# The last two steps of a triangular inverse: two chunks at a time, and six chunks at a time in one tile

## The chip, the cores and the metric

One core of a Trainium2 chip runs the whole program in one launch. The metric is the device time of an execution in microseconds (us). Before the change it is 3433.0 us, the median of three runs (3425.45, 3433.0 and 3433.71).

## The reference, cut to what matters

The reference is one layer of a hybrid encoder: RMSNorm, one wide projection `p = h @ w_in`, two recurrent mixers that share its columns, an output projection, a convolutional gated feed-forward part, a last RMSNorm. It runs over 2048 frames behind 16 meta tokens (one stream with zero state), and over 8 short streams of 16 frames with given states.

The change lies in the first mixer, RWKV-7 with 8 heads of 64. Per head and frame:

```python
def step(S, inp):
    r_t, k_t, v_t, w_t, kk_t, a_t = inp
    sa = jnp.einsum('bhvk,bhk->bhv', S, -kk_t)
    S = (S * w_t[:, :, None, :] + sa[..., None] * (kk_t * a_t)[:, :, None, :]
         + v_t[..., None] * k_t[:, :, None, :])
    return S, jnp.einsum('bhvk,bhk->bhv', S, r_t)
```

Taken 64 frames at a time (a chunk), the frames of a chunk depend on each other through a 64x64 triangular matrix L of products between keys, and the chunk needs the inverse of (1 + L). The reference never forms it; the kernel does.

## The kernel before, in words

**Layout.** The 2192 frames are split into segments: segment 0 has 272 (the eight short streams, the meta tokens and 128 frames), segments 1 to 5 have 384 each. A segment passes through the mixers in four units; a unit is one pair of RWKV heads (and beside it one head of the second mixer, mLSTM). A pair of heads fills the 128 partitions, 64 for each. So there are 24 units in all. A unit of segments 1 to 5 has six chunks, in three groups `cgroups` of two; a unit of segment 0 has five, of which the first group, the short streams, needs no last steps of the inverse.

**One unit.** `rwkv` makes the projections (`proj`, whose matmuls are line 322: 128x128 weights against 384 columns in float32r, three products for each of eight slices), the scores (tiles `scs`, line 710 to 733), and then the inverse. Its diagonal blocks of 16x16 are inverted on GpSimd (POOL, lines 751 to 760), go to memory and come back as the tile `ct`; lines 766 to 773 spread them into `TA`, six writes on POOL. `TA[:, 0]` holds the inverse so far and `TA[:, 1]` its transpose. Then `levels` (line 786) doubles the block size twice, 16 to 32 and 32 to 64, with the off-diagonal part of L masked into `cL`:

* `pi` = cL x TA0 (`mmd`: line 307, two matmuls of 64x64x64, one for each half of the partitions, each recorded as two instructions since they are float32),
* `wv` = a copy of `pi` out of PSUM, on VectorE (DVE),
* `pj` = TA1 x wv and, for the first doubling, also its transpose wv x TA1,
* TA = TA - pj, on DVE (line 804).

At its end line 808 applies the finished inverse to the chunk's keys and values (`pp`), and ScalarE (ACT) puts the result into `scs` (line 810). Then the chunks run one after another through the state `Z[u]` (lines 815 to 853, matmuls of lines 824, 837 and 843; the new state is line 841). In the code `levels` of a group stands ahead of that group's chunks and behind those of the group before.

**What sets the order.** A planner places the instructions of all engines by a priority that follows the order in the code, shifted by the offsets that `ranked`/`rank` add (`lev` adds 30, and -800 in segment 0), and by its own simulation of when each is ready. Each engine then runs its list in order. The chain of a unit (levels, chunks) is written out at the start of the next unit, ahead of that unit's front (`pend`, `at("chain")`), so the planner lays it between the next unit's projections.

**What is shared.** PSUM has eight banks; the tag `iv` has two. `pi`, `pj` and `pp` take them in turn, and so do the transposes of mLSTM (`m_T`, line 943) and those of the RWKV output (line 868). `TA` has three buffers of two chunks, `cL` and `wv` two each. POOL also issues the loads of the cached weights (line 372).

Of the kernel before, what the change touches and what calls it, by code (L numbers as in the profile page):

```python
# [211 lines left out]
def trunk_kernel(ctx: ExitStack, tc: tile.TileContext, A):  # L212
# [29 lines left out]
    def move(name, out, src, scale=None, eng="S"):  # L242
        e = knob(name, eng)
        turn[name] = turn.get(name, 0) + 1
        e = e[turn[name] % len(e)]
        if e == "S":
            if scale is None:
                S.copy(out, src)
            else:
                S.activation(out, src, AF.Copy, scale=scale)  # L250
        elif scale is None:
            (V if e == "V" else G).tensor_copy(out, src)
        else:
            (V if e == "V" else G).tensor_scalar(out, src, scale, None, op0=ALU.mult)

    def tt(name, out, a, b, op, eng="G"):
        e = knob(name, eng)
        turn[name] = turn.get(name, 0) + 1
        (V if e[turn[name] % len(e)] == "V" else G).tensor_tensor(out, a, b, op=op)  # L259
# [12 lines left out]
    def C(n, rows=128):  # L272
        o, w = COFF[n]
        return cst[:rows, o:o + w]
# [30 lines left out]
    def mmd(out, lhsT, rhs, start=True, stop=True):  # L305
        for h in (0, 64):
            T.matmul(out[h:h + 64], lhsT[h:h + 64], rhs[h:h + 64], start=start, stop=stop)  # L307
# [81 lines left out]
    def pt(tag, shape=(128, 512)):  # L389

        tag = knob("t_" + tag, tag.split("_")[0])
        t = psp.tile([128, 512], F32, name="ps_" + tag, tag=tag, bufs=banks[tag])[:, :math.prod(shape[1:])]
        if len(shape) == 2:
            return t
        return t.rearrange("p (a b) -> p a b", b=shape[2]) if len(shape) == 3 else t.rearrange("p (a b c) -> p a b c", b=shape[2], c=shape[3])

    with p1:
# [220 lines left out]
        def rwkv(u, s, ws, h, lo1, lo2):  # L618
# [127 lines left out]
            with rank("inv"):  # L746
                bt = sp.tile([48, 16, 16], F32, name="bt", tag="bt", bufs=1)
                nc.sync.dma_start(ad[:nch].rearrange("c p j -> p c j"), cm[:, :nch])
                nc.sync.dma_start(bt[:nb].rearrange("q i j -> q (i j)"), ad[:nch].rearrange("c (g i) j -> (c g) (i j)", i=16))
                tb = sp.tile([48, 2, 16, 16], F32, name="tb", tag="tb", bufs=1)  # L750
                tmp = sp.tile([48, 64], F32, name="ttmp", tag="ttmp", bufs=1)
                G.memset(tb[:nb, 0], 0.0)
                G.memset(tb[:nb, 0].rearrange("p i j -> p (i j)")[:, 0:256:17], 1.0)
                for j in range(15):
                    x, y = 15 - j, j + 1
                    tv = tmp[:nb, :x * y].rearrange("p (x y) -> p x y", y=y)
                    G.tensor_tensor(tv, bt[:nb, j, j + 1:].unsqueeze(2).to_broadcast([nb, x, y]),
                                    tb[:nb, 0, j, :y].unsqueeze(1).to_broadcast([nb, x, y]), op=ALU.mult)
                    G.tensor_tensor(tb[:nb, 0, j + 1:, :y], tb[:nb, 0, j + 1:, :y], tv, op=ALU.subtract)
                move("e_tb", tb[:nb, 1], tb[:nb, 0].rearrange("p i j -> p j i"), eng="G")  # L760
                td = dr.tile([2, nb, 256], F32, name=f"td{u}_{s}")
                nc.sync.dma_start(td[:].rearrange("a q e -> q a e"), tb[:nb].rearrange("p a i j -> p a (i j)"))
                ct = sp.tile([128, 2 * nch, 16], F32, name="ct", tag="ct", bufs=1)
                nc.sync.dma_start(ct, td[:].rearrange("a (c g) (i j) -> (g i) (a c) j", g=8, j=16))
                TAg = []
                for cg in cgroups:
                    TA = sp.tile([128, 2, 2, 64], F32, name="TA", tag="TA", bufs=KN.get("b_TA", 4))
                    TAg.append(TA)
                    k, c0 = len(cg), cg[0]
                    for a in range(2):  # L770
                        tt("e_TA", TA[:, a, :k].rearrange("p c (b j) -> p c b j", j=16),
                                        ct[:, a * nch + c0:a * nch + c0 + k].unsqueeze(2).to_broadcast([128, k, 4, 16]),
                                        C("seq4").unsqueeze(1).unsqueeze(3).to_broadcast([128, k, 4, 16]), ALU.mult)

            @ranked("chain")
            def chain():
# [4 lines left out]
                def sb(t, h):  # L781

                    return t[:, :, 64:320 if h else 192].rearrange("p c (j e) -> p c j e", j=2)[:, :, :, 0:64]

                @ranked("lev")
                def levels(cg, TA):
                    k, c0 = len(cg), cg[0]
                    if s > 0 or c0 > 0:
                        cL = sp.tile([128, 2, 2, 64], F32, name="cL", tag="cL", bufs=KN.get("b_cL", 2))
                        lev = C("lev").rearrange("p (l t) -> p l t", t=64)  # L790
                        for i, c in enumerate(cg):
                            tt("e_cL", cL[:, :, i], SC[c][:, 0:64].unsqueeze(1).to_broadcast([128, 2, 64]), lev, ALU.mult, eng="V")
                        for l in range(2):
                            pi = pt("iv", (128, 2, 2, 64))
                            for i, c in enumerate(cg):
                                mmd(pi[:, 0, i], cL[:, l, i], TA[:, 0, i])
                            wv = sp.tile([128, 2, 64], F32, name="wv", tag="wv")
                            move("e_wv", wv[:, :k], pi[:, 0, :k])
                            pj = pt("iv", (128, 2, 2, 64))
                            for i, c in enumerate(cg):  # L800
                                mmd(pj[:, 0, i], TA[:, 1, i], wv[:, i])
                                if l == 0:
                                    mmd(pj[:, 1, i], wv[:, i], TA[:, 1, i])
                            V.tensor_tensor(TA[:, :2 - l, :k], TA[:, :2 - l, :k], pj[:, :2 - l, :k], op=ALU.subtract)
                    pp = pt("iv", (128, 2, 128))
                    for i, c in enumerate(cg):
                        for h, hs in enumerate(HALF):
                            T.matmul(pp[hs, i], TA[hs, 0, i], sb(SC[c][hs].unsqueeze(1), h)[:, 0], start=True, stop=True)  # L808
                    for h, hs in enumerate(HALF):
                        move("e_pp", sb(SG[c0][hs, :k], h), pp[hs, :k].rearrange("p c (j d) -> p c j d", d=64), -1.0)  # L810

                for gi, cg in enumerate(cgroups):
                    levels(cg, TAg[gi])
                    smp = s == 0 and cg[0] == 0
                    for i, c in enumerate(cg):
                        sc = SC[c]
# [784 lines left out]
```

## Time and profile before

| | |
|---|---|
| median of three runs | 3433.0 us |
| the profiled execution's own time | 3429.68 us |
| its span in the trace | 3427.9 us |
| mean granted TensorE clock | 0.975 of full speed |
| busy share of the span | PE 97%, weight loads 89%, DVE 63%, ACT 35%, POOL 31% |

Times in the trace count from the start of the span. PE is TensorE's matmuls and PEld its weight loads. A matmul that follows another starts before that one has ended, so "busy" is not "at its peak": what a matmul costs is the step from its start to the start of the next. L307 is line 307 of the kernel. The mixers fill the span up to about 1900 us, the feed-forward part the rest.

### The profile page before, as it was taken

How to read it: one execution, taken by the hardware profiler on the slowest of the kernel's cores; microseconds unless marked ns; L12 is line 12 of the kernel's file. 1: busy time of each engine (PE TensorE's matmuls, PEld its weight loads, DVE VectorE, ACT ScalarE, POOL GpSimd, SP SyncE). 2: the span in 40 equal slices, each digit the busy share in tenths (PEclk: the TensorE clock that was granted, in tenths of full speed). 3: DMA queues.
4: the chain of work that ended last, by engine and by line, in shares of the span. 5: the costliest groups of instructions: out<-in, count | busy, mean ns of one | idle time of the engine just before them, and what ended most of it. 6: DMA issues, size and time to landing. Idle time of an engine off the chain costs nothing.

```text
span 3427.9 us, 62699 instructions
## 1 busy us (share of the span) xinstructions
PE 3330.3 (97%) x23700; PEld 3040.1 (89%) x23700; DVE 2151.2 (63%) x5475; ACT 1199.6 (35%) x2940; POOL 1059.2 (31%) x2408
## 2 busy tenths in 40 slices
PE   7999999999999999999999999999999999999998
PEld 6776887888888888888877999999999999999998
DVE  7777767666676676676665466657544557545454
ACT  5443435433343343334334333334222223222222
POOL 2432435434444434344341333333111113100002
PEclk9888999999999999999998999999999999999999
DMA  8753666455445545544643877775644445644445
GB/s 311 254 167 105 207 209 211 166 172 175 149 144 188 176 145 183 186 154 148 197 133 129 329 274 268 284 254 201 223 157 161 162 160 168 231 154 160 161 165 181
DMA packets 257150, 651.36 MB, mean 190 GB/s; under 512 B 73472, under 2 KB 139424, under 8 KB 217808
## 3 DMA queue, kind: packets, MB, share of 16 engines
q1 hardware_dynamic: 177768, 300.58, 27.4%
q0 software_dynamic: 35376, 225.64, 19.4%
q10 hardware_dynamic: 43704, 121.13, 9.1%
q8 instruction: 188, 3.08, 0.4%
q14 instruction: 114, 0.93, 0.1%
HBM read 491.33 MB, written 155.95 MB: 189 GB/s over the span
## 4 chain that ended last, share of the span: by engine, by line
PE 82%; DVE 8%; DMA 4%; ACT 2%; issue 2%; POOL 1%; SPq 0%; POOLq 0%; ACTq 0%; DVEq 0%
PE ps_gm L322 23%; PE ps_iv L1191 16%; PE ps_gm L1191 11%; PE ps_a L1191 8%; PE ps_m L1191 7%; PE ps_iv L307 2%; PE ps_a L710 2%; PE ps_ch L824 1%; PE ps_ch L843 1%; PE ps_ch L837 1%; PE ps_iv L808 1%; PE ps_m L953 1%; DMA xt<-in_x_dram 1%; PE ps_a L307 1%; PE ps_a L728 1%
## 5 line engine op out<-in xcount | busy, mean ns | idle before, releaser
L322 PE MATMUL ps_gm<-hhi,w 128*128 128x384 f32 (+1 forms) x2976 | 815.8, 346 | 7.2 <-DVE w L259 2.4
L322 PEld LDWEIGHTS ps_gm<-hhi,w 128*128 128x128 f32 x2976 | 543.0, 194 | 29.9 <-issue 5.5
L322 PE MATMUL ps_gm<-hlo,w 128*128 128x384 f32 (+1 forms) x1488 | 504.1, 339 | 3.0 <-DVE hlo L362 3.0
L1176 ACT CAST w<-wr 128x1024 fp32r<-128x1024 f32 (+3 forms) x180 | 166.6, 926 | 613.7 <-PE ps_iv L1191 533.1
L1191 PE MATMUL ps_iv<-gh,w 128*128 128x384 f32 (+1 forms) x1170 | 308.9, 329 | 3.9 <-ACT gh L1176 2.1
L1191 PE MATMUL ps_iv<-hs,w 128*128 128x384 f32 x1584 | 298.0, 336 | 2.6 <-DVE uu L1339 1.7
L322 PEld LDWEIGHTS ps_gm<-hlo,w 128*128 128x128 f32 x1488 | 288.8, 194 | 9.3 <-DVE hlo L362 3.4
L1191 PEld LDWEIGHTS ps_iv<-hs,w 128*128 128x128 f32 x1584 | 277.9, 188 | 4.2 <-DVE uu L1339 2.7
L1177 DVE TENSOR_TENSOR w<-wr,w 128x1024 fp32r<-128x1024 f32 (+3 forms) x180 | 199.3, 1107 | 110.4 <-ACT w L1176 107.2
L1191 PEld LDWEIGHTS ps_iv<-gh,w 128*128 128x128 f32 x1170 | 209.9, 188 | 5.1 <-ACT gh L1176 2.8
L1191 PE MATMUL ps_gm<-h,w 128*128 128x384 f32 x1056 | 202.7, 342 | 1.7 <-ACT p L1337 1.7
L1191 PE MATMUL ps_gm<-h2hi,w 128*128 128x384 f32 (+1 forms) x880 | 203.4, 315 | 0.1
L1277 DVE SCALAR_TENSOR_TENSOR ac<-ub,par,ac 128x384 f32<-128x384 f32 (+2 forms) x308 | 175.1, 601 | 31.5 <-ACT ac L1275 22.6
L1191 PE MATMUL ps_iv<-gw,w 128*128 128x384 f32 (+1 forms) x585 | 192.7, 329 | 1.9 <-POOL gw L1177 1.9
L1191 PEld LDWEIGHTS ps_gm<-h,w 128*128 128x128 f32 x1056 | 188.1, 189 | 2.1 <-ACT p L1337 2.0
L322 PE MATMUL ps_gm<-yhi,w 128*128 128x384 f32 (+1 forms) x640 | 168.5, 336 | 0.9 <-ACT yhi L361 0.7
L1425 DVE TENSOR_TENSOR x<-x,ps_iv 128x384 f32<-128x384 f32 (+1 forms) x160 | 84.4, 528 | 122.2 <-PE ps_iv L1191 121.2
L372 POOL DMA_DIRECT2D w<-wc x155 | 92.4, 596 | 222.2 <-PE ps_gm L322 176.4
L1191 PE MATMUL ps_m<-gh,w 128*128 128x384 f32 (+1 forms) x590 | 157.3, 329 | 0.0
L1191 PEld LDWEIGHTS ps_gm<-h2hi,w 128*128 128x128 f32 x880 | 150.9, 189 | 0.8 <-DVE w L1177 0.3
L1272 POOL COPY h_f<-ub 128x2 f32<-128x2 f32 x88 | 35.8, 406 | 366.1 <-DVE ub L1346 342.5
L1177 POOL TENSOR_TENSOR gw<-ac,gh 128x384 fp32r<-128x384 f32 x66 | 73.1, 1108 | 243.6 <-ACT gh L1176 243.6
(462 smaller groups left out, 7504.3 us busy)
## 6 DMA issues: line engine op xcount, KB each, us to landing
w<-wc POOLq DMA_DIRECT2D x155, 1024.0 KB, 5.3
wr<-ws SPq DMA_DIRECT2D x88, 512.0 KB, 4.2
w<-wg SPq DMA_DIRECT2D x44, 1024.0 KB, 6.7
wc<-w ACTq DMA_DIRECT2D x31, 1024.0 KB, 7.5
wr<-in_w_up_dram SPq DMA_DIRECT2D x52, 512.0 KB, 11.3
wg<-w ACTq DMA_DIRECT2D x22, 1024.0 KB, 6.9
ws<-ws POOLq DMA_DIRECT2D x44, 512.0 KB, 7.4
w<-wa SPq DMA_DIRECT2D x44, 512.0 KB
```

The lines of the kernel that those rows point to most:

```text
L307: T.matmul(out[h:h + 64], lhsT[h:h + 64], rhs[h:h + 64], start=start, stop=stop)
L322: T.matmul(ps, w, x, start=i == 0, stop=i == len(seq) - 1)
L372: nc.gpsimd.dma_start(w, WC[cache][:])
L710: T.matmul(psS[hs, i, X], kb[hs, X, cl(c)], ar[hs, h, :, cl(c)], start=True, stop=True)
L728: T.transpose(psT[:, j], src, ident)
L808: T.matmul(pp[hs, i], TA[hs, 0, i], sb(SC[c][hs].unsqueeze(1), h)[:, 0], start=True, stop=True)
L1176: S.copy(hi, src)
L1177: eng.tensor_tensor(lo, src, f32(hi), op=ALU.subtract)
L1191: ins = T.matmul(ps, l, r, start=start and i + j == 0, stop=stop and i == len(x) - 1 and j == 2, skip_group_check=not start)
L1272: G.tensor_copy(so_ffn[:, f, 8] if s == len(SEGS) - 1 else h_f[:, f], ub[:, n:n + 2])
L1277: V.scalar_tensor_tensor(av, view(i), PR("fw", i * 22 + f), av, op0=ALU.mult, op1=ALU.add)
L1425: V.tensor_tensor(X[s][:, d, :n], X[s][:, d, :n], p, op=ALU.add)
```

## The change

`TA` becomes one tile for all six chunks, with one buffer instead of three. `levels` is called once for a unit (in segment 0 once for its groups 1 and 2) and takes the two doublings for all chunks together: for each doubling `cL` is made by one instruction for each group, `pi` is one PSUM tile of up to six chunks, `wv` one copy of up to 384 columns. For the first doubling the two products go to two PSUM tiles, `first_` and `pj`, and two subtractions bring them into `TA`; the second has one. `cL` and `wv` have one buffer each. The application to keys and values is a function of its own, `apply`, called three times behind the doublings and, as the call stands inside `levels`, ahead of the first chunk; its instructions are the ones of before. The short streams' group calls `apply` alone.

```diff
--- before.py
+++ after.py
@@ -762,13 +762,11 @@
                 nc.sync.dma_start(td[:].rearrange("a q e -> q a e"), tb[:nb].rearrange("p a i j -> p a (i j)"))
                 ct = sp.tile([128, 2 * nch, 16], F32, name="ct", tag="ct", bufs=1)
                 nc.sync.dma_start(ct, td[:].rearrange("a (c g) (i j) -> (g i) (a c) j", g=8, j=16))
-                TAg = []
+                TA = sp.tile([128, 2, 6, 64], F32, name="TA", tag="TA", bufs=1)
                 for cg in cgroups:
-                    TA = sp.tile([128, 2, 2, 64], F32, name="TA", tag="TA", bufs=KN.get("b_TA", 4))
-                    TAg.append(TA)
                     k, c0 = len(cg), cg[0]
                     for a in range(2):
-                        tt("e_TA", TA[:, a, :k].rearrange("p c (b j) -> p c b j", j=16),
+                        tt("e_TA", TA[:, a, c0:c0 + k].rearrange("p c (b j) -> p c b j", j=16),
                                         ct[:, a * nch + c0:a * nch + c0 + k].unsqueeze(2).to_broadcast([128, k, 4, 16]),
                                         C("seq4").unsqueeze(1).unsqueeze(3).to_broadcast([128, k, 4, 16]), ALU.mult)
 
@@ -783,34 +781,52 @@
                     return t[:, :, 64:320 if h else 192].rearrange("p c (j e) -> p c j e", j=2)[:, :, :, 0:64]
 
                 @ranked("lev")
-                def levels(cg, TA):
-                    k, c0 = len(cg), cg[0]
-                    if s > 0 or c0 > 0:
-                        cL = sp.tile([128, 2, 2, 64], F32, name="cL", tag="cL", bufs=KN.get("b_cL", 2))
-                        lev = C("lev").rearrange("p (l t) -> p l t", t=64)
+                def levels():
+
+                    a = 2 if s == 0 else 0
+                    cs = slice(a, nch)
+                    lev = C("lev").rearrange("p (l t) -> p l t", t=64)
+                    for l in range(2):
+                        cL = sp.tile([128, 6, 64], F32, name="cL", tag="cL", bufs=1)
+                        for cg in cgroups:
+                            if cg[0] >= a:
+                                k = len(cg)
+                                tt("e_cL", cL[:, cg[0]:cg[0] + k], SG[cg[0]][:, :k, 0:64], lev[:, l:l + 1].to_broadcast([128, k, 64]), ALU.mult, eng="V")
+                        pi = pt("iv", (128, 6, 64))
+                        for c in range(a, nch):
+                            mmd(pi[:, c], cL[:, c], TA[:, 0, c])
+                        wv = sp.tile([128, 6, 64], F32, name="wv", tag="wv", bufs=1)
+                        move("e_wv", wv[:, cs], pi[:, cs])
+                        for x in range(2 - l):
+                            pj = pt("iv", (128, 6, 64))
+                            for c in range(a, nch):
+                                mmd(pj[:, c], *((wv[:, c], TA[:, 1, c]) if x else (TA[:, 1, c], wv[:, c])))
+                            if l == 0 and x == 0:
+                                first_ = pj
+                            elif l == 0:
+                                V.tensor_tensor(TA[:, 0, cs], TA[:, 0, cs], first_[:, cs], op=ALU.subtract)
+                                V.tensor_tensor(TA[:, 1, cs], TA[:, 1, cs], pj[:, cs], op=ALU.subtract)
+                            else:
+                                V.tensor_tensor(TA[:, 0, cs], TA[:, 0, cs], pj[:, cs], op=ALU.subtract)
+                    for cg in cgroups:
+                        if cg[0] >= a:
+                            apply(cg)
+
+                @ranked("lev")
+                def apply(cg):
+                        k, c0 = len(cg), cg[0]
+                        pp = pt("iv", (128, 2, 128))
                         for i, c in enumerate(cg):
-                            tt("e_cL", cL[:, :, i], SC[c][:, 0:64].unsqueeze(1).to_broadcast([128, 2, 64]), lev, ALU.mult, eng="V")
-                        for l in range(2):
-                            pi = pt("iv", (128, 2, 2, 64))
-                            for i, c in enumerate(cg):
-                                mmd(pi[:, 0, i], cL[:, l, i], TA[:, 0, i])
-                            wv = sp.tile([128, 2, 64], F32, name="wv", tag="wv")
-                            move("e_wv", wv[:, :k], pi[:, 0, :k])
-                            pj = pt("iv", (128, 2, 2, 64))
-                            for i, c in enumerate(cg):
-                                mmd(pj[:, 0, i], TA[:, 1, i], wv[:, i])
-                                if l == 0:
-                                    mmd(pj[:, 1, i], wv[:, i], TA[:, 1, i])
-                            V.tensor_tensor(TA[:, :2 - l, :k], TA[:, :2 - l, :k], pj[:, :2 - l, :k], op=ALU.subtract)
-                    pp = pt("iv", (128, 2, 128))
-                    for i, c in enumerate(cg):
+                            for h, hs in enumerate(HALF):
+                                T.matmul(pp[hs, i], TA[hs, 0, c], sb(SC[c][hs].unsqueeze(1), h)[:, 0], start=True, stop=True)
                         for h, hs in enumerate(HALF):
-                            T.matmul(pp[hs, i], TA[hs, 0, i], sb(SC[c][hs].unsqueeze(1), h)[:, 0], start=True, stop=True)
-                    for h, hs in enumerate(HALF):
-                        move("e_pp", sb(SG[c0][hs, :k], h), pp[hs, :k].rearrange("p c (j d) -> p c j d", d=64), -1.0)
-
-                for gi, cg in enumerate(cgroups):
-                    levels(cg, TAg[gi])
+                            move("e_pp", sb(SG[c0][hs, :k], h), pp[hs, :k].rearrange("p c (j d) -> p c j d", d=64), -1.0)
+
+                for cg in cgroups:
+                    if s == 0 and cg[0] == 0:
+                        apply(cg)
+                    elif cg[0] == (2 if s == 0 else 0):
+                        levels()
                     smp = s == 0 and cg[0] == 0
                     for i, c in enumerate(cg):
                         sc = SC[c]
```

## Rows read from the trace of the kernel before

**Rows 1.** The page, busy time of each engine, its share of the span and instructions.

```profile
PE 3330.3 (97%) x23700; PEld 3040.1 (89%) x23700; DVE 2151.2 (63%) x5475; ACT 1199.6 (35%) x2940; POOL 1059.2 (31%) x2408
```

**Rows 2.** Busy time by stretch: stretch, its length, engines, granted clock, DMA share, GB/s.

```profile
0.00:600.00 600.00, 557.17 (x4271) 456.93 (x4272) 438.01 (x1396) 261.63 (x737) 224.45 (x606) 0.91 0.61 209
600.00:1700.00 1100.00, 1084.20 (x8931) 925.11 (x8931) 734.55 (x2288) 410.64 (x1225) 455.55 (x1136) 0.99 0.52 167
1700.00:1900.00 200.00, 185.62 (x1538) 160.04 (x1537) 127.42 (x385) 81.11 (x214) 67.45 (x155) 0.93 0.45 145
1900.00:3428.00 1528.00, 1503.36 (x8967) 1498.00 (x8965) 851.25 (x1407) 446.19 (x764) 311.77 (x512) 0.99 0.59 205
```

**Rows 3.** Timeline of PE: start, length, engine, line, operation, tiles, count.

```profile
1343.60 0.68 PE L322 MATMUL ps_gm<-yhi,w 128*128 128x384 f32 x3
1344.22 0.45 PE L307 MATMUL ps_iv<-TA,cL 64*64 64x64 f32 x8
1344.60 0.45 PE L322 MATMUL ps_gm<-ylo,w 128*128 128x384 f32 x1
1344.88 0.34 PE L322 MATMUL ps_gm<-yhi,w 128*128 128x384 f32 x1
```

**Rows 4.** Timeline of PE, a batch behind other 64x64 work.

```profile
1354.96 0.60 PE L808 MATMUL ps_iv<-scs,TA 64*64 64x128 f32 x7
1355.29 0.50 PE L307 MATMUL ps_iv<-TA,cL 64*64 64x64 f32 x8
1355.72 0.55 PE L1016 MATMUL ps_m<-cst,nd 128*128 128x128 f32 x3
```

**Rows 5.** Timeline of PE, a batch of sixteen.

```profile
1329.30 0.33 PE L307 MATMUL ps_iv<-wv,TA 64*64 64x64 f32 x4
...
1329.69 0.28 PE L307 MATMUL ps_iv<-TA,wv 64*64 64x64 f32 x4
1329.91 0.33 PE L728 MATMUL ps_a<-cst,vm 128*128 128x128 f32 x1
```

**Rows 6.** Line 307 on PE, 1320 to 1372 us: count, shortest/median/longest ns, first, last.

```profile
L307 PE MATMUL ps_iv<-TA,cL x48: 216/218/267, 1323.8 to 1364.0; 64*64 64x64 f32 x48
L307 PE MATMUL ps_iv<-wv,TA x48: 216/218/268, 1329.3 to 1368.1; 64*64 64x64 f32 x48
L307 PE MATMUL ps_iv<-TA,wv x24: 218/218/219, 1329.5 to 1359.3; 64*64 64x64 f32 x24
```

**Rows 7.** Groups by form, 1300 to 1596 us: busy us, mean ns, idle before.

```profile
L252 DVE COPY pb<-ps_gm 128x384 f32<-128x384 f32 x14 | 7.7, 553 | 13.9 <-PE ps_gm L322 11.8 <-POOL ttmp L757 2.0
L252 DVE COPY wv<-ps_iv 128x128 f32<-128x128 f32 x25 | 7.2, 286 | 5.4 <-PE ps_iv L307 5.1
L259 POOL TENSOR_TENSOR cL<-scs,cst 128x128 f32<-128x128 f32 x12 | 5.7, 477 | 13.3 <-PE ps_iv L307 13.1
L804 DVE TENSOR_TENSOR TA<-TA,ps_iv 128x256 f32<-128x256 f32 x12 | 4.8, 403 | 0.4 <-PE ps_iv L307 0.3
L1039 DVE TENSOR_TENSOR xraw<-xraw,ps_gm 128x384 f32<-128x384 f32 x8 | 4.4, 547 | 4.4 <-PE ps_gm L322 4.4
L259 DVE TENSOR_TENSOR cL<-scs,cst 128x128 f32<-128x128 f32 x13 | 4.2, 320 | 0.0
L804 DVE TENSOR_TENSOR TA<-TA,ps_iv 128x128 f32<-128x128 f32 x12 | 3.4, 280 | 0.3 <-PE ps_iv L307 0.2
```

**Rows 8.** Tile TA over the span: its writes on POOL; idle time before instructions on it.

```profile
L259 POOL TENSOR_TENSOR TA<-ct,cst x144: 289/398/1268, 131.6 to 1811.1; 128x128 f32<-128x128 f32 x136, 128x64 f32<-128x64 f32 x8
...
  PE ps_iv L808: 11.6, 4
```

**Rows 9.** Line 841, 1340 to 1390 us.

```profile
L841 DVE SCALAR_TENSOR_TENSOR z<-ps_ch,pls,zf x6: 274/282/284, 1343.7 to 1388.8; 128x64 f32<-128x64 f32 x6
```

**Rows 10.** Timeline of PE, the last application of that unit.

```profile
1371.97 0.49 PE L808 MATMUL ps_iv<-scs,TA 64*64 64x128 f32 x6
```

**Rows 11.** Timeline of POOL, the next unit's writes of TA.

```profile
1382.00 2.67 POOL L259 TENSOR_TENSOR TA<-ct,cst 128x128 f32<-128x128 f32 x6
```

## The prediction

> **What bounds the kernel now.** I read the page's busy times first: the reader is to see PE at 97% of the span, and no other engine above 63% [rows 1]. PE is the candidate, but its busy time counts overlapping matmuls, so the next view is busy time by stretch [rows 2]. From 600 to 1700 us, where most units of segments 1 to 5 run through the mixers, PE idles 1100 - 1084.2 = 15.8 us at a granted clock of 0.99, while DVE is busy 734.55 us and POOL 455.55. Here the time is the sum of what PE's instructions cost, each from its start to the start of the next. The start (0 to 600) has 42.8 us of idle PE and a clock of 0.91, the end of the mixers (1700 to 1900) 14.4 us and 0.93; there a wait can show. From 1900 on the changed code doesn't run.
>
> The third view is PE's timeline, read for what a small matmul costs among large ones. Three large matmuls start at 1343.60, and at 0.17 us each the next would start near 1344.12; the batch of line 307 starts at 1344.22, so going over to it took 0.10 us. The batch of eight lasts until the next start at 1344.60, 0.38 us, and the large matmul behind it takes 0.28 us instead of 0.17, another 0.11 [rows 3]. Together 0.59 us. Inside a batch four instructions take about 0.11 us, 0.028 each (twelve start between 1329.30 and 1329.69, the first four slower) [rows 5], so the eight themselves are 0.22 us and **the change-over to them and back is 0.37 us**, more than the work.
>
> A batch behind other 64x64 work is different: line 307 follows line 808 after 0.33 us for seven instructions with 128 columns, without a gap, and leaves after 0.43 us [rows 4]. Its way back would be paid by line 808 if the batch weren't there. Taking it away saves the body at most, and the change doesn't take bodies away.
>
> **The change part by part.**
>
> *PE.* The matmuls stay: a unit has 48 + 48 + 24 = 120 records of line 307 [rows 6], six chunks times two halves times two records times five products, before and after. What changes is how they come. Before, three groups make four batches each (`pi`, `pj`, `pi`, `pj`), twelve in a unit, from 1323.8 to 1368.1 in the one shown [rows 6]. After, they come as four of 24 or 48 records: the two products of the first doubling wait for the same `wv`, so I take them as one batch. Eight batches go. Of the twelve in this unit nine stand as in rows 3, with large or other-shaped matmuls on both sides, and three beside other 64x64 work as in rows 4. In the next unit I count six and six. So the change-overs are 9 x 0.37 = 3.3 us in the one and 6 x 0.37 = 2.2 us in the other. After, four batches cost 4 x 0.37 = 1.5 us if all stand apart, and a third of the former cost (1.1 and 0.7 us) if they find neighbours as often. The saving is between 2.2 - 1.5 = 0.7 and 3.3 - 1.1 = 2.2 us a unit; I take the middle, 1.5. Twenty units give 30 us (bounds 14 and 44). Segment 0's four units go from eight batches to four, half of it: 3 us.
>
> *A rule to weigh.* The Trainium skill, TensorEngine Tiling, Key Properties, says that changing the tiling mode, not just the tile, drains TensorE. By that rule alone, with all twelve batches counted as two changes of mode, eight batches x 0.37 x 20 units + four x 0.37 x 4 would be 65 us. The trace agrees where the neighbour has another shape, and shows why not every batch counts: beside line 808 the mode is the same already [rows 4].
>
> *DVE and POOL.* `cL` stays six instructions of 128 columns a unit, three on each engine at 320 and 477 ns. Six copies to `wv` at 286 ns become two of 384 columns, which I price by the copy of that width, 553 ns; three subtractions at 403 and three at 280 become three at about 547, the price of a subtraction of that width from PSUM [rows 7]. DVE: 1.72 + 2.05 us become 1.11 + 1.64, one us a unit less. DVE is idle a third of the stretch [rows 2], so I cost it at nothing. If that cover were gone it would be a gain of 24 us.
>
> *The wait added.* The first chunk now waits for all six. Against group 0 alone its way is longer by the bodies (16 more records in three batches, 32 in the one that doubles: 80 x 0.028 = 2.2 us) and by the wider moves (2 x 0.27 for `wv`, 0.69 for two subtractions instead of one, 0.27 for the last: 1.5 us): **3.7 us later**. Behind that wait stand line 824 on PE and the state copies, but PE's list holds the next unit's projections there. Does the chain have room? Units follow each other every (1811.1 - 131.6) / 23 = 73 us [rows 8], and in the unit shown the chain goes from the first batch at 1323.8 [rows 6] to the last state at 1388.8 [rows 9]: 65 us. Eight us are free, so 3.7 are hidden, and the later chunks no longer wait for doublings of their own. At the end of the mixers nothing is left to lay between. There I charge 3 us once; bounds 0 and 8 (two units).
>
> *One buffer of TA, cL, wv.* POOL can't write `TA` of the next unit before the last `pp` of this one has read it. Before, it is the same for the last group: `pp` at 1371.97 [rows 10], the writes at 1382.00 [rows 11], 10 us apart. After, all three applications stand ahead of the first chunk, so the last reading comes earlier, not later. Cost nothing; the bound is a rival below. `cL` of the second doubling must wait for `pi` of the first, but it is wanted only after `wv`, `pj` and the subtractions.
>
> *The order.* A unit takes eight tiles of `iv` instead of fifteen, so mLSTM's transposes come to their bank sooner. The planner lays the whole program out anew, which I can't price from a row; I bound it by the idle time that PE has to give or to double, 16 us either way [rows 2], and take nothing.
>
> **Sum:** -30 - 3 + 3 = -30 us. The profiled execution took 3429.68 us, 3.3 below the median of 3433.0; the sum against it is 3399.7, so **3400 us**. The bounds: -44 - 3 - 16 gives 3367, and -14 - 1 + 8 + 16 gives 3439.
>
> **The rivals.**
>
> *The whole price of the change-overs:* the neighbours of the removed batches close up too, and each saves all of 0.37: eight in each of 20 units and four in each of 4 are 65 us. For it: nine of twelve stand apart in the unit shown. Against it: only six in the next. 3430 - 65 = 3365 us.
>
> *The batches don't stay together.* `cL` of the second doubling comes in three instructions, one on the slower engine, from one buffer; if the planner starts a product for each group as it comes, or if the 64x64 work that leaned on these batches now pays its own way in and out, the change-overs come back. For it: line 808 and the rest of the chain lean on line 307 in a quarter to half of the cases. Against: batches of sixteen stay whole today [rows 5]. A quarter of the saving is left, 8 us: 3422 us.
>
> *Slower: one TA blocks POOL.* POOL's list is in order; behind the six writes of `TA` stand the next unit's element-wise work and the issue of cached weights (line 372), for which the projections wait. POOL has already waited for line 808 before an instruction on `TA`, four times, 11.6 us, 2.9 each [rows 8]. If each of the 24 units did so and the projections came late by as much, 70 us are added and 33 saved: 3467 us. It decides from the point where the last `pp` of a unit falls behind the arrival of the next `ct`; before, 10 us were left [rows 10, 11]. Against it: the new order of the code puts that `pp` ahead of the chunks. The Trainium skill, Trainium Kernel Development and Optimization, Best Practices, tells to double-buffer for performance, which speaks for this rival, since three tiles lose their second buffer; the 10 us before speak against it here.
>
> **How the numbers follow.** The forecast (3400, own range 3383 to 3420) gets 0.56, the whole price 0.14, batches that come apart 0.16, the blocked POOL 0.14. A measurement of this kernel tells about 0.3%, 10 us, from no change. Faster by more: nearly all of the forecast (0.54), the whole price (0.14), and an eighth of the batches that come apart (0.02), 0.70. Within: most of that third case and the forecast's upper edge, 0.13. Slower: the blocked POOL and a bad order, 0.17. The range is 3370 to 3440: the bounds of the unknown costs, which leave out the lower edge of the first rival and most of the last.
>
> **What would show it.** In the timeline of 1300 to 1400 us, line 307 with `TA` and `cL` should come in runs of 24, with `wv` in one of 48 and one of 24, still 120 records a unit; the steps into and out of them unchanged, about 0.37 us for the pair. Groups by form: copies to `wv` of 128x384 near 553 ns and subtractions near 547. The units should follow each other in about 71.5 us instead of 73, with PE's idle time from 600 to 1700 about as small as before. The first chunk should start later behind the first batch than it does now. Wrong would be: runs of 8 as before (the second rival); POOL waiting for line 808 at the writes of `TA`, or PE waiting for weights (the third); more than 20 us of new idle time at the end of the mixers.

## The result and the profile after

The changed kernel takes 3462.3 us, the median of five runs (3444.48 to 3464.98), against 3431.92 of the kernel before in as many: a ratio of 1.0075, 95% interval 1.0053 to 1.0097. It is slower by 0.75%; the forecast was 3400 us and the range ended at 3440. The profiled execution, 3444.48 us, is the fastest of the five and has the highest granted clock of them, 0.967; the others have 0.961 to 0.965. What it shows of the clock's share is therefore probably the least of it.

The page's busy times, and busy time by stretch (the same columns as [rows 1, 2]):

```profile
PE 3326.8 (97%) x23700; PEld 3052.0 (89%) x23700; DVE 2138.7 (62%) x5325; ACT 1199.1 (35%) x2940; POOL 1076.4 (31%) x2410
```

```profile
0.00:600.00 600.00, 553.26 (x4382) 460.33 (x4383) 436.58 (x1379) 264.02 (x749) 235.99 (x620) 0.93 0.63 212
600.00:1700.00 1100.00, 1072.10 (x8763) 921.67 (x8762) 718.62 (x2170) 403.93 (x1204) 453.61 (x1123) 0.97 0.51 164
1700.00:1900.00 200.00, 183.81 (x1504) 156.59 (x1505) 121.81 (x353) 76.22 (x204) 66.56 (x145) 0.89 0.43 136
```

Against [rows 1] PE is busy 3.5 us less and idle 18 us more (3442.6 - 3326.8 = 115.8, before 97.6). From 600 to 1700 us it idles 27.9 us instead of 15.8, and the granted clock is 0.97 instead of 0.99 [rows 2]. In these 1100 us it got through 168 matmuls fewer. A mean clock below 1 is a mixture of the two levels, 1.00 (2.4 GHz) and 0.50 (1.2 GHz): over the span, 2 x (1 - 0.967) x 3442.6 = 227 us were at the lower one, before 2 x (1 - 0.975) x 3427.9 = 171.

To see what each of these is worth I took every step from one matmul's start to the next in both traces, and priced it by the mean step of the same pair of lines at full clock and without idle time, over both traces together. This splits the time between the first and the last start:

| us | before | after | difference |
|---|---|---|---|
| steps at their price | 3249.9 | 3235.6 | -14.3 |
| idle before a matmul | 78.6 | 96.6 | +18.0 |
| above the price, in stretches at a granted clock of 0.50 | 63.1 | 85.6 | +22.5 |
| rest (steps at full clock, above their price) | 16.9 | 5.2 | -11.7 |
| sum | 3408.5 | 3423.0 | +14.5 |

So steps were saved, 14 us by their price and 26 us with the rest, and more than that went to waits and to the clock.

The batches came out as planned but for the first. PE's timeline at the doublings of the unit that follows on [rows 3 to 6]:

```profile
1326.90 0.67 PE L307 MATMUL ps_iv<-TA,cL 64*64 64x64 f32 x14
1327.51 0.33 PE L884 MATMUL ps_iv<-cst,yn 128*128 128x128 f32 x1
1327.76 0.33 PE L307 MATMUL ps_iv<-TA,cL 64*64 64x64 f32 x2
1328.02 0.33 PE L884 MATMUL ps_iv<-cst,yn 128*128 128x128 f32 x1
1328.28 0.45 PE L307 MATMUL ps_iv<-TA,cL 64*64 64x64 f32 x8
...
1330.43 0.91 PE L307 MATMUL ps_iv<-wv,TA 64*64 64x64 f32 x24
1331.15 0.90 PE L307 MATMUL ps_iv<-TA,wv 64*64 64x64 f32 x24
1332.74 1.09 PE L710 MATMUL ps_a<-ar,kb 64*64 64x128 f32 x16 [0.70 <-ACT scs L248]
1333.77 0.55 PE L1032 MATMUL ps_m<-cst,nd 128*128 128x128 f32 x3
1334.24 0.92 PE L307 MATMUL ps_iv<-TA,cL 64*64 64x64 f32 x24
1335.09 0.44 PE L322 MATMUL ps_gm<-yhi,w 128*128 128x384 f32 x1
1335.37 0.34 PE L322 MATMUL ps_gm<-ylo,w 128*128 128x384 f32 x1
...
1337.49 0.91 PE L307 MATMUL ps_iv<-wv,TA 64*64 64x64 f32 x24
1339.20 1.09 PE L710 MATMUL ps_a<-ar,kb 64*64 64x128 f32 x16 [0.79 <-ACT scs L248]
1340.12 1.04 PE L821 MATMUL ps_iv<-scs,TA 64*64 64x128 f32 x16
```

Two products of 24 stand side by side as one batch of 48. But the first product, `TA` with `cL`, came apart into 14, 2 and 8, with transposes of the RWKV output (line 884, the old line 868) between the pieces. In the twenty units of segments 1 to 5 it came whole three times, in two pieces three times and in three pieces fourteen times, 51 pieces instead of 20.

What the prediction didn't see is beside the batches. The scores of the next unit (line 710) stood between the doublings before, too, and PE did not wait for them there:

```profile
1333.21 1.09 PE L710 MATMUL ps_a<-ar,kb 64*64 64x128 f32 x16
```

Now PE waits 0.70 and 0.79 us for ACT ahead of them (the bracket is the idle time and who ended it). From 1330.43 to 1335.09 no large matmul runs at all.

The other place is the border between two units. The same view, 1542.77 to 1552.34, and the stretches around it:

```profile
1542.77 0.34 PE L322 MATMUL ps_gm<-hhi,w 128*128 128x384 f32 x1
...
1544.54 0.33 PE L859 MATMUL ps_ch<-scs 64*64 64x64 f32 x2 [0.41 <-DVE scs L252]
1544.80 0.34 PE L853 MATMUL ps_ch<-scs 128*64 128x64 f32 x4
1545.06 0.33 PE L859 MATMUL ps_ch<-scs 64*64 64x64 f32 x2
1546.19 2.68 PE L710 MATMUL ps_a<-ar,kb 64*64 64x128 f32 x16 [0.81 <-DVE ar L259]
...
1551.39 0.84 PE L322 MATMUL ps_gm<-hhi,w 128*128 128x384 f32 x2
1552.03 0.47 PE L322 MATMUL ps_gm<-hlo,w 128*128 128x384 f32 x1
```

```profile
1540.00:1545.30 5.30, 4.89 (x43) 4.07 (x41) 3.62 (x13) 1.38 (x4) 4.47 (x9) 1.00 0.14 17
1545.50:1552.20 6.70, 5.95 (x33) 4.91 (x34) 5.61 (x20) 2.79 (x6) 1.73 (x3) 0.50 0.35 139
1552.40:1558.00 5.60, 5.60 (x51) 4.97 (x50) 4.59 (x18) 3.27 (x13) 1.14 (x4) 1.00 0.01 1
```

Behind the product at 1542.77 PE has only small matmuls, of the last chunks, of mLSTM and of the next scores, and waits 0.41 us for DVE. At 1545.47 the granted clock falls to 0.50, 0.1 us into the second wait. Now sixteen matmuls of line 710 take 2.6 us (1546.19 to 1548.80) instead of 0.9 (1339.20 to 1340.12), and a large one 0.32 (1551.39 to 1552.03 for two) instead of 0.17. The kernel before has borders as long without a product of line 322. They hold no wait, and besides small matmuls they have eight records of 384 columns (lines 625, 629, 633 and 741, two each). Behind the first of these two the clock holds, behind the second it falls:

```profile
1528.50:1535.60 7.10, 7.10 (x55) 4.15 (x53) 5.69 (x21) 3.71 (x12) 3.45 (x10) 1.00 0.57 163
...
1382.33:1388.23 5.90, 5.90 (x53) 3.26 (x52) 5.50 (x18) 1.59 (x4) 3.39 (x9) 1.00 0.39 108
1388.40:1391.80 3.40, 3.40 (x11) 3.40 (x12) 3.39 (x9) 1.11 (x3) 1.21 (x2) 0.50 0.27 101
```

From 600 to 1700 us the clock is at 0.50 four times in the trace before and thirteen times in the one after, 20.5 and 75.1 us in all. Ten of the thirteen begin within 12 us of the front of a unit (line 625). A wait is not needed for it: at five of the thirteen, and two of the four before, PE had not idled for 7 us when they began. The Trainium skill, TensorE: Matmul & The Clock Gate, Part 1, says that the lower clock is the default and activity releases it. The trace agrees in so far as the clock is back at 1.00 at 1552.30, after large products have run from 1550.58 on. Which small work counts how much, no run here shows.

PE's waits from 600 to 1700 us, who waited for whom, us in total, times, longest; after, and then two of the lines before:

```profile
PE ps_ch L859 <- DVE scs L252: 7.3, 6, 2.6
PE ps_iv L307 <- DVE wv L252: 4.4, 3, 2.4
PE ps_a L710 <- ACT scs L248: 4.4, 6, 1.0
```

```profile
PE ps_a L710 <- ACT scs L248: 3.3, 4, 1.2
...
PE ps_iv L307 <- DVE wv L252: 0.8, 2, 0.5
```

Line 859 is the old line 843, the matmul that completes a chunk's output. PE waits there for DVE's copy of the chunk's first product out of PSUM, 7.3 us; before, that wait isn't among the eleven longest of the stretch.

### The profile page after: what moved, and what is told of

It reads as the page before. It is cut to its first block, busy times and chain, and to the rows that moved or that the text cites. A ratio compares the mean times of both kernels' runs of the same rounds, so it can differ in the third digit from the quotient of the medians.

```text
span 3442.6 us, 62491 instructions
## 1 busy us (share of the span) xinstructions
PE 3326.8 (97%) x23700; PEld 3052.0 (89%) x23700; DVE 2138.7 (62%) x5325; ACT 1199.1 (35%) x2940; POOL 1076.4 (31%) x2410
## 4 chain that ended last, share of the span: by engine, by line
PE 81%; DVE 9%; DMA 3%; POOL 3%; issue 2%; ACT 2%; SPq 0%; POOLq 0%; DVEq 0%; ACTq 0%
PE ps_gm L322 23%; PE ps_iv L1207 16%; PE ps_gm L1207 10%; PE ps_a L1207 8%; PE ps_m L1207 7%; PE ps_iv L307 2%; PE ps_a L710 2%; PE ps_ch L840 1%; PE ps_ch L859 1%; PE ps_ch L853 1%; PE ps_iv L821 1%; DMA wr<-in_w_up_dram 1%; DMA wraw<-in_w_in_dram 1%; PE ps_m L969 1%; POOL ttmp L757 1%
## 5 line engine op out<-in xcount | busy, mean ns | idle before, releaser
L1293 DVE SCALAR_TENSOR_TENSOR ac<-ub,par,ac 128x384 f32<-128x384 f32 (+2 forms) x308 | 176.1, 606 | 34.8 <-ACT ac L1291 23.9
```

The lines of the kernel that those rows point to most:

```text
L1293: V.scalar_tensor_tensor(av, view(i), PR("fw", i * 22 + f), av, op0=ALU.mult, op1=ALU.add)
```

## The experiments

All ratios are to the kernel before, run on the same chip in the same session, with a 95% interval. The idle time of PE from 600 to 1700 us is 1100 less the first busy time of the stretch's row, and beside it stands the time in that stretch at a granted clock of 0.50 (before 15.8 and 20.5 us). Both come from one profiled execution of each kernel, which can be any of its runs: e2's is the slowest of four. The clock is the median of the runs (before 0.975 to 0.976, 0.971 to 0.979 singly).

| kernel | ratio | interval | idle us | us at 0.50 | clock |
|---|---|---|---|---|---|
| the change | 1.0075 | 1.0053 to 1.0097 | 27.9 | 75.1 | 0.962 |
| e1 all doublings first, not merged | 1.0038 | 1.0025 to 1.0052 | 19.1 | 20.5 | 0.974 |
| e2 merged, applications as before | 1.0094 | 1.0078 to 1.0111 | 41.3 | 64.9 | 0.968 |
| e3, e4 before, offset 20 and 40 | 1.0002, 1.0016 | 0.9988 to 1.0016, 1.0002 to 1.0029 | 19.4, 14.8 | 34.1, 23.9 | 0.976, 0.975 |
| e5 the change, more large matmuls | 1.0110 | 1.0095 to 1.0126 | 16.2 | 37.5 | 0.970 |
| e6 before, more large matmuls | 1.0108 | 1.0082 to 1.0135 | 15.2 | 20.5 | 0.974 |
| e7, e12 two chunks, then four; offset 30, 80 | 1.0050, 1.0049 | 1.0033 to 1.0067, 1.0029 to 1.0068 | 20.5, 23.8 | 54.6, 34.1 | 0.970, 0.970 |
| e8, e9, e10, e11 the change, offset -100, 0, 80, 200 | 1.0170, 1.0099, 1.0087, 1.0150 | all within 1.0064 to 1.0187 | 52.2, 33.4, 34.9, 28.3 | 64.9, 68.3, 64.9, 95.6 | 0.966, 0.967, 0.966, 0.960 |
| e13 one tile, not merged | 1.0034 | 1.0011 to 1.0057 | 15.0 | 37.5 | 0.968 |
| e14 merged, moves by group | 1.0046 | 1.0028 to 1.0063 | 29.7 | 54.6 | 0.968 |

**e1, the order alone.** In the kernel before, all groups' `levels` are called ahead of the first chunk:

```diff
-                    levels(cg, TAg[gi])
+                    if gi == 0 or (s == 0 and gi == 1):
+                        for gj in ([0] if s == 0 and gi == 0 else range(gi, 3)):
+                            levels(cgroups[gj], TAg[gj])
```

> The kernel before, doublings still for each group of two chunks in their own tiles, but all groups' doublings and applications stand ahead of the unit's first chunk. Theory 1 (bunching: the small work is drawn together ahead of the first chunk and the chunks slide into the stretch between two units, where few large matmuls are left; PE idles more and the clock falls more often): slower than before although no batch is merged, 3445 to 3475 us, granted clock 0.960 to 0.968 against 0.975, idle PE over 105 us of the span. Theory 2 (the long merged batches themselves bring the clock down): as before, 3425 to 3437, clock 0.973 to 0.977. Theory 3 (any new layout of the planner moves the time by such amounts): can lie anywhere from 3410 to 3465.

Measured: 3441.95 us, between the two theories. Its stretch:

```profile
600.00:1700.00 1100.00, 1080.86 (x8874) 916.60 (x8873) 726.45 (x2276) 408.92 (x1216) 453.56 (x1139) 0.99 0.51 166
```

This order costs 0.38%, some 13 us, with nearly the clock of the kernel before. It can't be read as half of the change's harm: from one matmul to the next PE changes its tile shape (64\*64, 128\*128 and so on) 1768 times in this trace, against 1698 before and 1580 in the change. Thirty-five pairs more, at 0.37 us, are an estimate of 13 us by themselves, and the merged kernel doesn't pay them.

**e2, the merge with the old place of the applications.**

```diff
-                    for cg in cgroups:
-                        if cg[0] >= a:
-                            apply(cg)
...
+                    if cg[0] == (2 if s == 0 else 0):
                         levels()
+                    apply(cg)
```

> The changed kernel, doublings merged for all six chunks, but each group's application stands ahead of its own two chunks again instead of ahead of the first. Theory 1: the doublings still stand together, two applications of three move away from the bunch: between the changed kernel and the one before, 3435 to 3460 us, clock 0.962 to 0.972. Theory 2: as the changed kernel, 3444 to 3465, clock 0.961 to 0.967. Theory 3: anywhere from 3410 to 3465.

Measured: 3461.39 us. Theory 1 expected relief and there is none, so drawing the applications ahead isn't what hurts. The median clock, 0.968, is above the change's 0.962 and in theory 1's range; the time is in theory 2's.

```profile
600.00:1700.00 1100.00, 1058.69 (x8656) 903.24 (x8655) 711.32 (x2128) 404.87 (x1212) 439.00 (x1118) 0.97 0.49 161
```

**e3 and e4, a new layout alone.** `'lev': 30` becomes 20 and 40 in the kernel before.

> The kernel before with the planner's offset of the doublings at 20 instead of 30; same instructions, a new layout. Theories 1 and 2: no bunch is made, within 0.3% of before, 3422 to 3442 us, clock 0.972 to 0.978. Theory 3 (a new layout alone is worth 20 to 30 us): off by more than 10 us in one of the two runs of this kind.

> The kernel before with the planner's offset of the doublings at 40 instead of 30; same instructions, a new layout. Theories 1 and 2: within 0.3% of before, 3422 to 3442 us, clock 0.972 to 0.978. Theory 3: off by more than 10 us in one of the two runs of this kind.

Measured: 3428.88 and 3432.89 us, both within 0.3%. These two layouts move the kernel before by 0.02 and 0.16%, and the change's 0.75% is outside both intervals. They are small shifts, though: in the changed kernel larger ones move the time much more (e8 to e11).

**e5 and e6, large matmuls at the border.** In the change, and in the kernel before as a control, ahead of line 625:

```diff
+            for k_ in range(8):
+                T.matmul(pw[:, :SEGS[s][1]], ws[2][0][:, k_], h[0][:, k_, :SEGS[s][1]], start=True, stop=True)
             T.matmul(pw[:, :m], lw2[0:64, 0, us], lo1[0:64, :m], start=True, stop=True)
```

> The changed kernel with eight more large matmuls (128x128 against the segment's columns) in each unit, into the bank of line 625 just ahead of it, where they are overwritten: at the border between two units, where the granted clock falls. Added work: 24 x 8 x 0.17 = 33 us at full clock. Theory 1 (the clock is lost where the stretch between units holds small matmuls and waits but no large ones): the clock rises from 0.961-0.967 to 0.972 or more, the added work is paid back in good part, 3445 to 3475 us. Theory 2 (the long batches of the doublings bring it down): clock unchanged, the 33 us come on top, 3480 to 3500.

> The kernel before with the same eight large matmuls in each unit, the control of the run before this one. Both theories: little clock to win back (0.975), so most of 33 us is added, 3448 to 3465 us, clock 0.976 to 0.981.

Measured: 3465.14 and 3468.05 us. The kernel before pays 1.08%, 37 us, for the 33 us of work, a little above the range expected, and its clock, 0.974, is below the 0.976 expected. The changed kernel pays 1.10 - 0.75 = 0.35%, 12 us, for the same work: some 25 us come back, about 13 us either way if the three intervals are taken together. With the filling the two kernels are equal within their intervals. The stretches, of the change with it and of the control:

```profile
600.00:1700.00 1100.00, 1083.80 (x8905) 932.58 (x8904) 718.58 (x2149) 411.08 (x1223) 441.12 (x1133) 0.98 0.51 166
```

```profile
600.00:1700.00 1100.00, 1084.83 (x8921) 926.37 (x8920) 717.55 (x2260) 407.07 (x1215) 442.71 (x1117) 0.99 0.50 164
```

Idle PE is back at the old level (16.2 and 15.2 us). The change's clock rose from 0.962 to 0.970, short of the 0.972 expected, and the time at 0.50 in the stretch halved, from 75.1 to 37.5 us, where the control has 20.5. Work of no use costs the changed kernel a third of what it costs the other, so what the change loses is time in which PE waits or runs at the lower clock. That the border is the place for it is not shown: the filling was tried nowhere else, and it gives the planner a new layout, too.

**e7 and e12, a smaller merge.** The first two chunks' doublings alone, the other four together ahead of the third chunk; e12 with offset 80.

```diff
-                def levels():
+                def levels(gs):
...
-                        levels()
+                    elif s > 0 and cg[0] == 0:
+                        levels(cgroups[:1])
+                    elif s > 0 and cg[0] == 2:
+                        levels(cgroups[1:])
```

> The changed kernel, but in segments 1 to 5 the doublings of the first two chunks are done alone, ahead of the first chunk, and those of the other four together, ahead of the third; one tile TA as in the change. Eight batches a unit instead of four, twelve before. Theory 1 (bunching ahead of the first chunk): most of the harm is gone and half of the saved change-overs stays, 3412 to 3432 us, idle PE from 600 to 1700 under 20 us, clock 0.972 to 0.977. Theory 2 (length of a batch): half of the harm stays, 3432 to 3448, clock 0.966 to 0.972.

> The kernel with the first two chunks doubled alone and the other four together, offset 80 instead of 30. Theory A: as that kernel at 30, 3438 to 3452 us. Theory B: later is better, 3415 to 3435 us.

Measured: 3445.18 and 3450.14 us. Theory 1's 3412 to 3432 is missed: the first chunk no longer waits for six, and two thirds of the harm remain, with a clock of 0.970, as theory 2 said. How the harm goes with the number of chunks merged is not shown by it: e13, which merges nothing, keeps 0.34%, and the intervals overlap. At offset 80 it is theory A's time.

**e8 to e11, the offset of the merged doublings.** `'lev': 30` becomes -100, 0, 80 and 200 in the change.

> The changed kernel with the planner's offset of doublings and applications at -100 instead of 30, so that they are placed before other work as soon as they are ready; same instructions. Theory 1 (the chunks end too late, in the border between units): the chain starts and ends some 10 us earlier in a unit, less idle PE, 3425 to 3445 us, clock 0.970 or more. Theory 2: as the changed kernel, 3444 to 3465, clock 0.961 to 0.967.

> The changed kernel with the planner's offset of doublings and applications at 0 instead of 30. The run at -100 was slower than the change. Theory A (the harm lies in the merge: four large bunches of small work per unit, wherever they are put): within 0.5% of the changed kernel, 3445 to 3475 us. Theory B (the harm lies in an offset that no longer fits, and earlier is worse): between the changed kernel and the one at -100, 3455 to 3480 us.

> The changed kernel with that offset at 80 instead of 30: the bunches are placed later, behind more of the projections. Theory A: 3440 to 3470 us, slower than before. Theory B: later is better, 3415 to 3440 us, idle PE from 600 to 1700 under 22 us, clock 0.970 or more.

> The changed kernel with that offset at 200. Theory A: 3440 to 3480 us, slower than before. Theory B: 3405 to 3440 us, unless the chunks then end so late that the border between units holds only small work; in that case slower than at 80.

Measured: 3487.1, 3466.6, 3465.51 and 3487.15 us. I had expected an early chain to help at -100; the harm is the greatest there, and PE idles 52 us:

```profile
600.00:1700.00 1100.00, 1047.77 (x8550) 893.64 (x8550) 694.33 (x2103) 399.04 (x1182) 433.76 (x1087) 0.97 0.49 159
```

But the chain did not come early. By the traces the first batch starts 25.1 us behind the line 625 ahead of it at -100 and 23.7 us in the change, and the last state comes 72.6 us behind that batch instead of 65.4 (medians of the twenty units of segments 1 to 5). So this run, whose time is outside both ranges, does not test whether the chunks end too late, and that stays open. At 200 idle time is low, the clock is the lowest, 0.960, and the time is above theory A's range; theory B had allowed for a harm at 200, if the border then holds only small work. What stands is that no offset tried makes the merge pay.

**e13, one tile without the merge.** `levels([cg])` for each group ahead of its chunks, with the change's `TA`, `cL` and `wv` of one buffer:

```diff
-                    elif cg[0] == (2 if s == 0 else 0):
-                        levels()
+                    else:
+                        levels([cg])
```

> The changed kernel with its single TA, cL and wv and its two PSUM tiles for the first doubling, but the doublings done for each group of two chunks ahead of that group's chunks, as before. If the harm lies in the merge, none is left: 3422 to 3442 us, clock 0.973 to 0.978, idle PE from 600 to 1700 under 21 us. If it lies in the single buffers (a group's cL, wv or TA waiting for the one before), it stays: 3445 to 3470 us.

**e14, the merge with moves by group.**

```diff
-                        move("e_wv", wv[:, cs], pi[:, cs])
+                        for g_ in gsl:
+                            move("e_wv", wv[:, g_], pi[:, g_])
...
-                                V.tensor_tensor(TA[:, 0, cs], TA[:, 0, cs], pj[:, cs], op=ALU.subtract)
+                                for g_ in gsl:
+                                    V.tensor_tensor(TA[:, 0, g_], TA[:, 0, g_], pj[:, g_], op=ALU.subtract)
```

(the other two subtractions likewise).

> The changed kernel with its matmuls in the same order, but the copies to wv and the subtractions made for each group of two chunks again (128 columns each), so that a group's product can start when its own part is there. If the harm comes from the wide moves, behind which a batch of 24 or 48 waits as a whole, much of it goes: 3425 to 3450 us, clock 0.970 or more. If it comes from all doublings standing together ahead of the first chunk, whatever the moves, it stays: 3450 to 3475 us, clock 0.961 to 0.968.

Measured: 3439.17 and 3443.55 us. Their stretches:

```profile
600.00:1700.00 1100.00, 1085.00 (x8933) 931.39 (x8929) 737.78 (x2330) 413.31 (x1224) 452.43 (x1147) 0.98 0.52 168
```

```profile
600.00:1700.00 1100.00, 1070.30 (x8769) 916.68 (x8768) 723.03 (x2305) 406.02 (x1214) 449.04 (x1137) 0.98 0.51 165
```

Without the merge the idle time is the old one, 15.0 us: the additional idle time comes with the merge. But e13's clock is 0.968, not the 0.973 expected, and 0.34% stay. Two thirds of its additional time at 0.50 lie in the first 600 us (139.9 us there, against 105.8 before), the rest in the stretch to 1700 (37.5 against 20.5). Why one tile should cost clock I can't say from these runs. In e14 the idle time stays at 29.7 us, so it doesn't come from the wide moves. For the time the run decides nothing: 3443.55 us lies in the range of the wide moves, the clock in that of the doublings that stand together, and the interval overlaps the change's.

## Why the prediction was wrong

**The step that failed** is the part on the order: "I bound it by the idle time that PE has to give or to double, 16 us either way, and take nothing". In that stretch the idle time rose by 12 us, inside the bound; over the span it rose by 18, where the sum had nothing. And the sum had no term at all for the granted clock, though [rows 2] show 0.91, 0.99 and 0.93 by stretch and so a price. The clock cost 22.5 us in the fastest run. The median run is 18 us slower than that one, at a clock of 0.962 instead of 0.967: 2 x 0.005 x 3460 = 35 us more at the lower level, where a large matmul takes 0.32 us instead of 0.17, so some 16 us more by this estimate. In e5 and e6, with more large matmuls in both kernels, some 25 us of this come back.

**The saving was mis-sized.** I took 33 us, 89 pairs of change-overs, from nine and six isolated batches of twelve in two units. In the traces PE changes its tile shape 1698 times before and 1580 times after, which is 59 pairs, 22 us at 0.37. The steps give 14 us by their price and 26 with the rest; with the filling on both sides, where idle time is nearly equal, the same pricing gives 3281 and 3269 us, a saving of 12. The price of one change-over comes out much the same in a batch of 24: it lasts 0.85 us from 1334.24 on, against 24 x 0.028 = 0.67, and the large matmul behind it takes 0.28 instead of 0.17, so 0.18 and 0.11 us besides the way in, where [rows 3] have 0.16 and 0.11. What I overcounted is how many vanish. The first batch came apart, 31 pieces more than planned, at most 11 us at 0.37. The second rival had batches that come apart, but not this one and not for this reason: it named the second doubling's `cL` coming group by group, and pieces of 14, 2 and 8 are no groups of 8. Its other half, that the 64x64 work that leaned on a batch now pays its own way, I have not priced by itself. The Trainium skill's rule (TensorEngine Tiling, Key Properties), that a change of the tiling mode drains TensorE, with every batch counted had given 65 us, three times what the changes of shape come to.

**Right:** 120 records a unit, the batches of 24 and 48 behind the first product, and the wide moves on DVE (554 ns for the copy, 547, 542 and 554 for the three subtractions from 1300 to 1604 us, against 553 and 547):

```profile
L252 DVE COPY wv<-ps_iv 128x384 f32<-128x384 f32 x8 | 4.4, 554 | 0.6 <-PE ps_iv L307 0.5
L810 DVE TENSOR_TENSOR TA<-TA,ps_iv 128x384 f32<-128x384 f32 x4 | 2.2, 554 | 5.3 <-PE ps_iv L307 5.3
L807 DVE TENSOR_TENSOR TA<-TA,ps_iv 128x384 f32<-128x384 f32 x4 | 2.2, 547 | 0.0
L808 DVE TENSOR_TENSOR TA<-TA,ps_iv 128x384 f32<-128x384 f32 x4 | 2.2, 542 | 0.0
```

**The late first chunk** was right. In the unit shown its state comes at 1344.6, 17.7 us behind the first batch at 1326.9, where it was 19.9 us before [rows 6, 9], but that unit is the exception. Over the twenty units of segments 1 to 5 the median went from 21.2 to 23.9 us, 2.7 us later where I had 3.7, and the last state comes 65.4 us behind the first batch instead of 65.0. The delay is covered by the end of the chain, as forecast. Still, units follow each other every (1819.0 - 128.5) / 23 = 73.5 us instead of the 71.5 forecast:

```profile
L259 POOL TENSOR_TENSOR TA<-ct,cst x144: 286/394/1381, 128.5 to 1819.0; 128x128 f32<-128x128 f32 x136, 128x64 f32<-128x64 f32 x8
```

**The slower rival named the wrong mechanism.** POOL no longer waits for the application before an instruction on `TA`: where [rows 8] have 11.6 us, the same view after names line 821 nowhere on POOL. The side was right by accident only. The Trainium skill's advice to double-buffer (Trainium Kernel Development and Optimization, Best Practices) speaks of overlapping DMA with compute, and POOL and DVE write these three tiles; the trace doesn't bear it out here, though e13's 0.34% is open.

**What is settled and what is not.** Shown: change-overs are saved; where all six chunks are merged, PE idles more (27.9 to 52.2 us of the stretch, against 14.8 to 19.4 in the kernels that merge nothing) and is longer at the lower clock (54.6 to 95.6 us against 20.5 to 37.5), unless large matmuls are added; no offset tried cures it; with the added large matmuls the two kernels take the same time. Not shown: how much of the 0.75% is the merge's own, since e13 keeps 0.34% without it and its interval touches the change's; that the layout alone does nothing, since e3 and e4 shifted it by little, and offsets alone take the changed kernel from 1.0075 to 1.0170; that the filling must stand at the border. Argued only: that the planner, having bunched the doublings, leaves less large work for the border. The cause of the waits and of the lower clock stays open to that extent. I did not find a version that beats the kernel before.

## What to carry to other kernels

In this kernel PE is full, and the small batches lay between large matmuls, which covered most of their waits. Merging them saved change-overs (0.37 us for a pair), but PE then waited more and ran longer at the lower clock, and that cost more than was saved. Put the granted clock into the sum as a term of its own, by stretch, before calling a kernel bound by the count of PE's steps. To find out whether a loss is one of clock and waits, add useless large work in both kernels: what it costs the one less than the other is loss that it filled. Add it in a second place, too, before naming the place. And count over all units before reading one: the unit shown here was an exception in where its first chunk came.

## What the runs showed that I had not expected

Adding 192 large matmuls, 33 us of work at full clock, cost the changed kernel 12 us and the kernel before 37.

Two borders of the kernel before, 1528.50 to 1535.60 and 1382.33 to 1388.23, have no product of line 322 and no wait of PE; the clock stayed at 1.00 behind the one and fell to 0.50 behind the other. A full PE does not by itself keep the clock.
